# Gathering tokens for eight experts at a time in a two-layer mixture-of-experts trunk

## The chip, the cores and the metric

The kernel runs on one core of a Trainium2 chip. What is measured is the device time of one execution in microseconds (us): three runs of the kernel before took 750.36, 750.12 and 752.44 us, so the median is 750.36 us. One further execution was recorded by the hardware profiler; it took 750.05 us, of which 748.3 us lie between its first and its last instruction (the span). All times in the profile are counted from the start of that span.

A core has engines that run side by side, each with a queue of its own that it works through strictly in order: TensorE (PE in the profile: matmuls, into PSUM), VectorE (DVE) and ScalarE (ACT, both elementwise), GpSimd (POOL), and SyncE (SP), which here only issues transfers (DMA). Instructions of different engines wait for each other by semaphores.

## The reference

Two layers (l = 0, 1) act on 256 tokens of 1024 features in float32. With six modulation vectors made from a conditioning vector by a large product (`ada_w`), each layer does:

```
h = rmsnorm(x) * (1 + sc1) + sh1
x = x + g1 * (concat(three kinds of attention on h @ w_in) @ w_out)       # the mixer
h = rmsnorm(x) * (1 + sc2) + sh2
x = x + g2 * moe(h)                                                       # 16 experts
return rmsnorm(x)                                                         # after layer 1
```

The router picks one of four groups of experts for each token and the two best experts in it. The output of an expert is `(silu(h @ w_gate) * (h @ w_up) * gate) @ w_down`, with 512 inner features. All sixteen experts get tokens, so all their weights have to be read, some 200 MB of the 283.63 MB that the whole kernel moves.

## The kernel before

**Weights.** All large weights go by one SP queue, in an order fixed when the program is built (`Ring.fill`, L154), in units of 512 KB (a tile of 128x1024). Most units go into a ring of 29 tiles named `big`. A unit of the ring can be issued when the unit 29 places back in the ring has been released, that is, read for the last time by PE. Some units are put elsewhere: for units 21 to 26 of each layer's experts (`HALVES`) two tiles of the pool `w` are used, and for those in `LENT` a tile of the pool `k`. Units in other pools take no place in the ring. As SP issues in order, a unit that waits holds up all units behind it. At most eight transfers are under way at a time: a full queue makes SP wait for a transfer to end.

**The experts.** `moe` goes through the 16 experts as eight pairs (j = 0 to 7). A pair has eight units for its gate products, eight for up and eight for down. I count the units of one layer's experts r = 0, 1, 2, ...: gate of pair 0 is 0 to 7, up of pair 0 is 8 to 15, gate of pair 1 is 16 to 23, down of pair 0 is 24 to 31, up of pair 1 is 32 to 39 and so on. `first` (L1362) makes a quarter of a gate or up product and releases two units; `down` (L1408) does the same for the way back; `combine` (L1429) spreads the result to the tokens' rows. In a trace one float32 matmul is two records, so a `first` is eight records of L1362; the order lists count it as four.

**The gather.** Each expert has 64 places. `pos` says, for each token and expert, which place it has. `one_hot(b)` (L1304, DVE) makes a 0/1 matrix of 128 tokens x (4 experts x 64 places) for each half of the tokens. `gather(b, k2)` (L1328) multiplies the normed tokens, split into a rounded part `xhi` and a rest `xlo`, with it: the result for 2 of the 8 blocks k of 128 features fills one PSUM tile `t`. There are two such tiles. `modulate` then writes scale * t + shift into a `k` tile, for two blocks at a time alternately by ACT (L724) and DVE (L726). With four experts in a gather there are four gathers in a layer, at pairs 0, 2, 4 and 6. Two of their quarters stand ahead of the pair's first `first`, one between the first and the second and one between the second and the third.

**What sets the order.** Each engine works in the order in which the Python code emits its instructions, but for some pieces that are kept back on purpose (`issue_after`). Ahead of the experts the router's DVE instructions come in this order: `pos` (L1239), the one-hot matrix, the eight pieces of `xlo` (L1247), small ones for the gate weights, and the sum `g2rows` (L1297), from which `g2` (L562) makes the factor of the expert layer's output by two float32 matmuls. The mixer's steps follow a list (`MIX`, `TAIL`), where a letter d stands for a quarter of the product for one modulation vector (`one_unit`, L532, eight records), CF for a piece of attention kind C, AM for one of kind A, and W for a step of the output projection. The products of projections are three matmuls each (L718 to L720), on weights that ACT and DVE split first (L770, L775).

**The end.** The last pair's way back (`last`, L1443 and L1460) is cut into pieces. For the final norm, POOL multiplies x with the final gains (`weigh`, L1570), and after the norm's factor is known, DVE and ACT multiply by it (L1564, L1562); four transfers of 256 KB write the output.

Of the kernel before, what the change touches and what calls it, by code (L numbers as in the profile page):

```python
# [29 lines left out]
SCRATCH = 512  # L30
AHEAD = 2
HALVES = ((21, 27), (21, 27))
LENT = (((27, 32), (61, 62), (64, 65), (67, 68)),) * 2
NW = 17
A_START = 24

# [19 lines left out]

START = ["X c c R c c S00".split(), "S00 S01 X0 X1 a S02 X2 a X3 a a R a".split()]
TAIL = """
CT0 d CT1 d CF0 AM1 d d W0 CF1
BV0 BV1 W1 BV2 BV3 BO0 BV4 W2 BV5 CV0 W3 BO1 CV1 CV2 W4 CO0 W5 W6  # L60
"""
MIX = [("""
# [137 lines left out]
class Body:  # L200
# [20 lines left out]
    def setup(self):  # L221
        nc, a, const = self.nc, self.a, self.const
        cb = self.cb = const.tile([128, NCONST], F32, name="cb")
        nc.sync.dma_start(out=cb[:, 0:C_Z], in_=a["first"])
        self.load_x()
        self.ring.fill(2 * KT + 4)
        nc.sync.dma_start(out=cb[:, C_CAUSAL:C_CAUSAL2], in_=a["rest"])

        self.qb = const.tile([128, 512], F32, name="qb")
        nc.gpsimd.memset(self.qb, 0.0)  # L230
        for l in range(DEPTH):
            nc.gpsimd.dma_start(out=self.qb[l:128:32], in_=a["ada_b"][l])
# [12 lines left out]
        self.cact = cb[:, _AT["C"]]  # L245
        nc.scalar.activation(self.cact, self.cact, AF.Silu)
        cols = cb[:, _AT["COLS"]].rearrange("p (n k) -> p n k", k=KT)
        self.bcol = cols[:, 0:6 * DEPTH].rearrange("p (l v) k -> p l v k", l=DEPTH)
        self.gain = {nm: cols[:, 6 * DEPTH + DEPTH * i:6 * DEPTH + DEPTH * (i + 1)]
                     for i, nm in enumerate(("norm_mix_g", "norm_ffn_g"))}  # L250
        self.add = cb[:, _AT["ADD"]]
        self.pair = cb[:, _AT["PAIR"]]
        self.subg = cb[:, _AT["SUBG"]].rearrange("p (l d) -> p l d", l=DEPTH)
        self.sink = cb[:, _AT["SINK"]].rearrange("p (l d) -> p l d", l=DEPTH)
        self.wr = cb[:, _AT["WR"]].rearrange("p (l k g) -> p l k g", l=DEPTH, k=KT)
        self.rb = [cb[0:1, _AT["RB"]][:, 20 * l:20 * l + 20] for l in range(DEPTH)]
        self.tables(posi)
        self.later = True
# [58 lines left out]
    def lambdas(self):  # L317
# [8 lines left out]
        nc.vector.tensor_tensor(out=lam, in0=ls[:, 1], in1=ls[:, 0], op=OP.subtract)  # L326
        for l in range(DEPTH):
            nc.vector.tensor_scalar(lam[:, l:l + 1], lam[:, l:l + 1], -self.lambda_init(l), None, op0=OP.add)
        pl = self.pt.tile([128, 512], F32, name="t")
        nc.tensor.matmul(pl[:, 0:DEPTH], lhsT=self.ones[0:1], rhs=lam[0:1, :], start=True, stop=True)  # L330
# [119 lines left out]
    def ada_unit(self, l, q, i):  # L450
# [15 lines left out]
        else:  # L466
            nc.scalar.copy(rows[64:128], self.q[64:128])
            nc.vector.tensor_tensor(out=rows[0:64], in0=self.q[0:64], in1=self.qb[0:64], op=OP.add)
        self.pending.append(lambda: self.ada_columns(l, q, rows))

    def ada_columns(self, l, q, rows):
        nc = self.nc
# [83 lines left out]
    def g2(self, l):  # L556
# [338 lines left out]
    def mixer(self, l):  # L895
# [17 lines left out]

        if self.later:
            self.more_tables()


        def proj(u, g):
# [229 lines left out]
        for what in MIX[l]:  # L1148
# [11 lines left out]
                self.spread(l, int(n))  # L1160
            elif name == "L":
                if self.later:
                    self.lambdas()
                    self.later = False
            else:
                steps[name](int(n))
# [88 lines left out]
    def gates_of_tokens(self, l, dense, lg, l5, rank, og, tl):  # L1255
# [35 lines left out]
        if not dense:  # L1291
# [1 line left out]
            nc.gpsimd.tensor_copy(ghl[:, :, 0], gate)  # L1293
            nc.gpsimd.tensor_tensor(out=ghl[:, :, 1], in0=gate, in1=ghl[:, :, 0].bitcast(F32), op=OP.subtract)
            self.ghl = ghl
        self.g2rows = self.w()
        nc.vector.tensor_tensor(out=self.g2rows, in0=self.q, in1=self.qb, op=OP.add)  # L1297

    def one_hot(self, b):

        one = self.w(F32R).rearrange("p (t e s) -> p t e s", t=2, e=4)
        iota = self.cb[:, C_IOTA:C_IOTA + CAP].unsqueeze(1).to_broadcast([128, 4, CAP])
        for t in range(2):
            i = self.nc.vector.tensor_tensor(out=one[:, t], in0=iota, op=OP.is_equal,  # L1304
                                             in1=self.pos[:, t, 4 * b:4 * b + 4].unsqueeze(2).to_broadcast([128, 4, CAP]))
        self.hot[b] = one.rearrange("p t e s -> p t (e s)")
        return i


    def moe(self, l):  # L1310
        nc, ring = self.nc, self.ring
        hot = self.hot
        sh, sc, g = self.mod[l, 3], self.mod[l, 4], None
        xt, G, U, pts, gates, act = {}, {}, {}, {}, {}, {}

        def gather(b, k2):

            if k2 == 0:
                if b:
                    self.one_hot(b)  # L1320
                xt[b] = [self.wk.tile([128, 4, S], F32, name="k") for _ in range(2)]
            one = hot[b]
            p = self.pt.tile([128, 512], F32, name="t").rearrange("p (k s) -> p k s", k=2)
            for kk in range(2):
                n = 0
                for part in (self.xhi, self.xlo):
                    for t in range(2):
                        nc.tensor.matmul(p[:, kk], lhsT=part[t][:, 2 * k2 + kk], rhs=one[:, t],  # L1328
                                         start=(n == 0), stop=(n == 3))
                        n += 1  # L1330
            for kk in range(2):
                self.modulate(xt[b][k2 // 2][:, 2 * (k2 % 2) + kk], p[:, kk], sc, sh, 2 * k2 + kk, 1 - k2 % 2)

        def places(j):

            p = self.pt.tile([128, 512], F32, name="t")
            hf = hot[j // 2][:, :, 128 * (j % 2):128 * (j % 2) + 128]
# [14 lines left out]
        def first(kind, store, j, hh):  # L1352

            if hh == 0:
                store[j] = self.ps.tile([128, 512], F32, name="s")
            x = xt[j // 2]
            w = [ring.take2((kind, l, 2 * j + u, hh)) for u in range(2)]
            for kk in range(2):
                k = 2 * hh + kk
                for u in range(2):  # L1360
                    c = (j % 2) * 128 + 64 * u
                    nc.tensor.matmul(store[j][64 * u:64 * u + 64, :], lhsT=x[k // 4][:, k % 4, c:c + 64],  # L1362
                                     rhs=w[u][kk], start=(k == 0), stop=(k == KT - 1))
            ring.done(2)

        def gates_of(j, between=None):

            if j % 2:
                first("gate", G, j, 0)
                first("gate", G, j, 1)  # L1370
                if between:
                    between()
            else:
                gather(j // 2, 0)
                gather(j // 2, 1)
                first("gate", G, j, 0)
                gather(j // 2, 2)
                if between:
                    between()
                first("gate", G, j, 1)  # L1380
                gather(j // 2, 3)
            first("gate", G, j, 2)
            first("gate", G, j, 3)
            silu(j)
# [48 lines left out]
        def last(j):  # L1433
# [18 lines left out]
            def combined(d, c0, n):  # L1452
# [12 lines left out]
                        nc.vector.tensor_tensor(out=self.x[t][:, c], in0=self.x[t][:, c], in1=o[t], op=OP.add)  # L1465
                else:
                    self.key = nc.vector.tensor_tensor(out=self.xt[:, :, c], in0=self.xt[:, :, c], in1=o3, op=OP.add)
                if l + 1 == DEPTH:
                    self.weigh(c)
                i = {0: 0, 512: 2, 768: 1}[c0]  # L1470
                for t in range(2):
# [22 lines left out]
                    next(self.starting)  # L1494

        for j in range(8):
            gates_of(j, (lambda: down_in(j - 1)) if j else None)
            if j == 0:
                self.g2(l)
                g = self.mod[l, 5]  # L1500
            if j:
                parts = down(j - 1)
            places(j)
            for hh in range(4):
                first("up", U, j, hh)
            product(j)
# [47 lines left out]
    def final(self, out):  # L1554
        nc = self.nc
        r = self.rstds(self.squares(), False)
        for t in range(2):
            for hf in range(2):
                c = slice(512 * hf, 512 * hf + 512)
                y = self.y[t][:, c]  # L1560
                if t and hf:
                    nc.scalar.activation(y, y, AF.Copy, scale=r[t])  # L1562
                else:
                    nc.vector.tensor_scalar(y, y, r[t], None, op0=OP.mult)  # L1564
                (nc.scalar if hf else nc.sync).dma_start(out=out[0, 128 * t:128 * t + 128, c], in_=y)

    def weigh(self, c):

# [12 lines left out]
    def forward(self, out, dense):  # L1581
# [14 lines left out]
                self.moe(l)  # L1596
        if dense:
            self.load_fng()
            self.weigh(slice(0, D))
        self.final(out)  # L1600


# [49 lines left out]
```

## Time and profile before

| | |
|---|---|
| median of three runs | 750.36 us |
| profiled execution | 750.05 us |
| its span | 748.3 us |
| mean granted clock of TensorE | 0.986 of full speed |
| PE busy | 711.3 us (95%) |
| DVE, ACT, POOL busy | 342.1, 211.5, 65.3 us |
| moved | 283.63 MB, mean 379 GB/s |
| transfers of 512 KB, issue to landing | 10.2 us median |

The table is an account over the whole span. Layer 0's mixer fills it up to about 166 us, its experts up to about 381 us; layer 1's mixer follows up to about 523 us and its experts up to about 737 us. The rate at which data moves, in 40 slices of the span, tells the stages apart better than any sum: it is near 409 GB/s in most slices and well below it in a few.

### The profile page before, as it was taken

What the parts mean: (1) busy time and instruction counts of PE and PEld (TensorE: products, weight loads), DVE (VectorE), ACT (ScalarE), POOL (GpSimd) and SP (SyncE); (2) the same over time, 40 slices, a digit from 0 to 9 for tenths busy, and PEclk for the clock granted to TensorE, in tenths of its full rate; (3) what the DMA queues carried; (4) which work ended last, traced back from release to release, by engine and by line L of the source; (5) the groups of instructions that cost most, each with busy time, mean ns of one, the idle gap of its engine ahead of it and who ended that gap; (6) DMA issues with size and microseconds to landing.
All of it is one profiled execution on the core that took longest, in us unless ns stands there. A gap on an engine that the chain in (4) does not pass through costs nothing. (4 is left out here: it accounts for less than half of the span.)

```text
span 748.3 us, 10676 instructions
## 1 busy us (share of the span) xinstructions
PE 711.3 (95%) x3790; PEld 368.8 (49%) x3790; DVE 342.1 (46%) x940; ACT 211.5 (28%) x482; POOL 65.3 (9%) x89
## 2 busy tenths in 40 slices
PE   6899899989999999999999999898999999999993
PEld 2565675754353353343337677575435335344341
DVE  4587697373133133223358879538213312332234
ACT  2345345532111111111134645544211011112011
POOL 1010224101000000000001122400100000000002
PEclk9999999999999999999999999999999999999997
DMA  9999999999999999999999996869989999999991
GB/s 352 409 410 406 406 410 408 408 386 409 391 357 409 409 410 409 408 409 410 397 408 409 406 406 210 335 209 401 327 339 396 409 409 409 409 409 409 409 379 63
DMA packets 82745, 283.63 MB, mean 379 GB/s; under 512 B 9198, under 2 KB 9327, under 8 KB 82684
## 3 DMA queue, kind: packets, MB, share of 16 engines
q1 hardware_dynamic: 82186, 282.33, 96.1%
q8 instruction: 32, 0.52, 0.3%
q10 hardware_dynamic: 434, 0.53, 0.2%
q14 instruction: 29, 0.24, 0.1%
q0 software_dynamic: 64, 0.02, 0.0%
HBM read 281.78 MB, written 1.06 MB: 378 GB/s over the span
## 5 line engine op out<-in xcount | busy, mean ns | idle before, releaser
L1362 PE MATMUL s<-big,k 128*64 128x512 f32 x976 | 228.2, 598 | 0.0
L1362 PEld LDWEIGHTS s<-big,k 128*64 128x64 f32 x976 | 67.4, 136 | 118.5 <-issue 103.2
L1414 DVE SCALAR_TENSOR_TENSOR w<-acc,gs,g 128x512 f32<-128x512 f32 x28 | 21.0, 751 | 155.3 <-PE acc L1408 153.8
L1408 PE MATMUL acc<-big,w 128*64 128x512 f32 x384 | 84.4, 592 | 0.0
L775 DVE TENSOR_TENSOR k<-big,k 128x1024 fp32r<-128x1024 f32 (+1 forms) x56 | 66.4, 1192 | 14.5 <-ACT k L770 10.2
L718 PE MATMUL acc<-k 128*128 128x512 f32 (+1 forms) x176 | 70.0, 397 | 3.0 <-ACT k L707 2.0
L720 PE MATMUL acc<-k 128*128 128x512 f32 (+1 forms) x176 | 66.6, 379 | 0.0
L719 PE MATMUL acc<-k 128*128 128x512 f32 (+1 forms) x176 | 66.3, 377 | 0.0
L770 ACT CAST k<-big 128x1024 fp32r<-128x1024 f32 (+1 forms) x56 | 54.2, 985 | 37.3 <-PE acc L719 27.5
L1408 PEld LDWEIGHTS acc<-big,w 128*64 128x64 f32 x384 | 27.6, 137 | 54.8 <-issue 52.2
L1393 DVE TENSOR_TENSOR w<-w,s 128x512 f32<-128x512 f32 x16 | 11.0, 688 | 84.3 <-PE s L1362 84.3
L718 PEld LDWEIGHTS acc<-k 128*128 128x128 f32 x176 | 33.9, 193 | 18.2 <-issue 6.1
L1418 ACT CAST w<-w 128x512 fp32r<-128x512 f32 x28 | 17.3, 618 | 89.8 <-DVE w L1414 89.8
L1328 PEld LDWEIGHTS t<-w,k 128*128 128x128 f32 x256 | 32.8, 190 | 16.3 <-issue 9.9
L835 ACT ACTIVATE w<-w,nm 128x128 f32<-128x128 f32 (+1 forms) x80 | 35.4, 444 | 15.9 <-DVE nm L833 15.8
L1399 ACT COPY w<-t 128x512 f32<-128x512 f32 x16 | 9.4, 585 | 107.9 <-PE t L803 107.9
L1328 PE MATMUL t<-w,k 128*128 128x256 f32 x256 | 37.6, 291 | 1.7 <-DVE w L1304 1.7
L724 ACT ACTIVATE k<-t,mod,mod 128x256 f32<-128x256 f32 x32 | 16.3, 561 | 79.1 <-PE t L1328 79.1
L720 PEld LDWEIGHTS acc<-k 128*128 128x128 f32 x176 | 33.7, 191 | 7.7 <-DVE k L891 1.6
L719 PEld LDWEIGHTS acc<-k 128*128 128x128 f32 x176 | 33.9, 193 | 5.0
L803 PE MATMUL t<-cb,w 128*128 128x128 f32 x224 | 34.1, 281 | 1.4 <-ACT w L860 1.4
L1431 DVE TENSOR_TENSOR x<-x,acc 128x512 f32<-128x512 f32 x56 | 34.9, 681 | 0.2
(269 smaller groups left out, 852.6 us busy)
## 6 DMA issues: line engine op xcount, KB each, us to landing
big<-in_expert_w_up_dram SPq DMA_DIRECT2D x126, 512.0 KB, 10.2
big<-in_expert_w_gate_dram SPq DMA_DIRECT2D x118, 512.0 KB, 10.2
big<-in_expert_w_down_dram SPq DMA_DIRECT2D x108, 512.0 KB, 10.1
big<-in_ada_w_dram SPq DMA_DIRECT2D x80, 512.0 KB, 10.2
big<-in_w_in_dram SPq DMA_DIRECT2D x32, 512.0 KB, 10.2
big<-in_ada_w_first_dram SPq DMA_DIRECT2D x16, 512.0 KB, 10.2
big<-in_w_out_dram SPq DMA_DIRECT2D x16, 512.0 KB, 9.7
w<-in_expert_w_down_dram SPq DMA_DIRECT2D x20, 256.0 KB, 6.8
```

The lines of the kernel that those rows point to most:

```text
L718: self.nc.tensor.matmul(p, lhsT=xh, rhs=wh, start=start, stop=False)
L719: self.nc.tensor.matmul(p, lhsT=xh, rhs=wl, start=False, stop=False)
L720: self.nc.tensor.matmul(p, lhsT=xl, rhs=wh, start=False, stop=stop)
L770: nc.scalar.copy(hi, w)
L775: nc.vector.tensor_tensor(out=lo, in0=w, in1=hi.bitcast(F32), op=OP.subtract)
L803: self.nc.tensor.transpose(p[:, i], b, self.ident)
L835: nc.scalar.activation(e[:, h], e[:, h], AF.Exp, bias=nm[:, g:g + 1], scale=scale, accum_out=sm[:, g:g + 1])
L1328: nc.tensor.matmul(p[:, kk], lhsT=part[t][:, 2 * k2 + kk], rhs=one[:, t], start=(n == 0), stop=(n == 3))
L1362: nc.tensor.matmul(store[j][64 * u:64 * u + 64, :], lhsT=x[k // 4][:, k % 4, c:c + 64], rhs=w[u][kk], start=(k == 0), stop=(k == KT - 1))
L1408: nc.tensor.matmul(ps[hf][64 * u:64 * u + 64, :], lhsT=act[j][:, f, 64 * u:64 * u + 64], rhs=w[u][hf], start=(f == 0), stop=(f == 3))
L1414: nc.vector.scalar_tensor_tensor(out=ds[-1], in0=p, scalar=gates[j], in1=g[:, 512 * hf:512 * hf + 512], op0=OP.mult, op1=OP.mult)
L1431: nc.vector.tensor_tensor(out=self.x[t][:, c], in0=self.x[t][:, c], in1=p, op=OP.add)
```

## The change

`one_hot(b)` now makes the matrix for eight experts (two instructions of 128x512), and `gather(b, k)` fills a PSUM tile with one block k of features for all eight. There are two gathers in a layer, at pairs 0 and 4, of eight blocks each: four blocks stand ahead of the pair's first `first`, two between the first and the second, two between the second and the third. `modulate` now takes one block of 128x512, even blocks by ACT and odd blocks by DVE. The gathered tokens take four `k` tiles where they took two, and `LENT` gives units 30 and 31 back to the ring. The 0/1 rows that `places` needs are made for each pair by `rows_of`. `g2` works with two rounded parts (four matmuls in place of two float32 ones). In the mixer, the columns of a modulation vector (`ada_columns`) come one stage later, the lambdas of attention kind A are computed earlier, and in `TAIL` one d moves ahead of CF0. At the end, POOL weighs only the first 512 columns, DVE does the rest in one instruction per half of the tokens, and two transfers of 512 KB write the output.

```
-LENT = (((27, 32), (61, 62), (64, 65), (67, 68)),) * 2
+LENT = (((27, 30), (61, 62), (64, 65), (67, 68)),) * 2
-CT0 d CT1 d CF0 AM1 d d W0 CF1
+CT0 d CT1 d d CF0 AM1 d W0 CF1
...
-        self.add = cb[:, _AT["ADD"]]
+        self.add = const.tile([128, 2 * DEPTH], F32R, name="add")
+        nc.gpsimd.tensor_copy(self.add, cb[:, _AT["ADD"]])
...
-        self.pending.append(lambda: self.ada_columns(l, q, rows))
+        self.pending.append(lambda: self.pending.append(lambda: self.ada_columns(l, q, rows)))
...
         if self.later:
             self.more_tables()
+            self.lambdas()
...
-            nc.tensor.matmul(p, lhsT=self.add[:, 2 * l + h:2 * l + h + 1].to_broadcast([128, 128]), rhs=self.g2rows,
-                             start=True, stop=True)
+            for n, part in enumerate(self.g2rows):
+                nc.tensor.matmul(p, lhsT=self.add[:, 2 * l + h:2 * l + h + 1].to_broadcast([128, 128]), rhs=part,
+                                 start=(n == 0), stop=(n == 1))
...
-        self.g2rows = self.w()
-        nc.vector.tensor_tensor(out=self.g2rows, in0=self.q, in1=self.qb, op=OP.add)
+        rows = self.w()
+        nc.vector.tensor_tensor(out=rows, in0=self.q, in1=self.qb, op=OP.add)
+        self.g2rows = [self.w(F32R) for _ in range(2)]
+        nc.scalar.copy(self.g2rows[0], rows)
+        nc.vector.tensor_tensor(out=self.g2rows[1], in0=rows, in1=self.g2rows[0].bitcast(F32), op=OP.subtract)
...
+        def gather(b, k):
+            if k == 0:
+                xt[b] = []
+            if k % 2 == 0:
+                xt[b].append(self.wk.tile([128, 2, 512], F32, name="k"))
+            p = self.pt.tile([128, 512], F32, name="t")
+            n = 0
+            for part in (self.xhi, self.xlo):
+                for t in range(2):
+                    nc.tensor.matmul(p, lhsT=part[t][:, k], rhs=hot[b][t], start=(n == 0), stop=(n == 3))
+                    n += 1
+            self.modulate(xt[b][k // 2][:, k % 2], p, sc, sh, k, 1 - k % 2)
...
+            ks = range(KT) if j % 4 == 0 else ()
+            for k in ks[0:4]:
+                gather(j // 4, k)
+            first("gate", G, j, 0)
+            for k in ks[4:6]:
+                gather(j // 4, k)
+            if between and ks:
+                between()
+            first("gate", G, j, 1)
+            if between and not ks:
+                between()
+            for k in ks[6:8]:
+                gather(j // 4, k)
             first("gate", G, j, 2)
             first("gate", G, j, 3)
...
-                if l + 1 == DEPTH:
+                if l + 1 == DEPTH and c0 == 0:
                     self.weigh(c)
...
+            y = self.y[t]
+            nc.scalar.activation(y[:, c0], y[:, c0], AF.Copy, scale=r[t])
+            nc.vector.scalar_tensor_tensor(out=y[:, c1], in0=self.x[t][:, c1], scalar=r[t], in1=self.fng[:, c1],
+                                           op0=OP.mult, op1=OP.mult)
+            nc.sync.dma_start(out=out[0, 128 * t:128 * t + 128, :], in_=y)
```

The first place is DVE at the start of layer 0's experts in the kernel before. The names `k<-t` are modulations of gathered tokens, `w<-cb,pos` is the one-hot matrix and `w<-s,qb` the sum for g2.

```order
314 L1304 TENSOR_TENSOR w<-cb,pos 128x256 x2
315 L1247 SCALAR_TENSOR_TENSOR k<-x,newton,k 128x256 x8
316 L1260 TENSOR_REDUCE mp<-pos 128x1
319 L1267 TENSOR_SCALAR o_1883<-rank 128x32
320 L1297 TENSOR_TENSOR w<-s,qb 128x512
321 L726 TENSOR_SCALAR k<-t,mod_4_1429,mod_3_891 128x256 x2
325 L1270 TENSOR_REDUCE m_1882<-g_1888 128x8
326 L1282 RECIPROCAL w_1899<-w_1899 128x8
327 L726 TENSOR_SCALAR k<-t,mod_4_1429,mod_3_891 128x256 x2
```

DVE's first modulation stands behind the sum for g2; it is that of blocks 2 and 3. The same place of DVE after the change:

```order
316 L1318 TENSOR_TENSOR w<-cb,pos 128x512 x2
317 L1254 SCALAR_TENSOR_TENSOR k<-x,newton,k 128x256 x8
318 L1267 TENSOR_REDUCE mp<-pos 128x1
321 L1274 TENSOR_SCALAR o_1882<-rank 128x32
322 L1304 TENSOR_TENSOR w<-s,qb 128x512
323 L1268 TENSOR_SCALAR ovf<-mp 128x1
324 L732 TENSOR_SCALAR k<-t,mod_4_1421,mod_3_918 128x512
327 L1307 TENSOR_TENSOR w<-w 128x512
329 L732 TENSOR_SCALAR k<-t,mod_4_1421,mod_3_918 128x512
330 L1289 RECIPROCAL w_1898<-w_1898 128x8
331 L732 TENSOR_SCALAR k<-t,mod_4_1421,mod_3_918 128x512 x2
```

The first modulation still stands behind the sum for g2, and it is now that of block 1. On PE the same place reads, before:

```order
416 L1328 MATMUL t<-w,k 128x256 x16
417 L1362 MATMUL s<-big,k 64x512 x4
418 L1328 MATMUL t<-w,k 128x256 x8
419 L1362 MATMUL s<-big,k 64x512 x4
422 L562 MATMUL acc<-w,cb 128x512 x2
```

After, PE has as many matmuls, of twice the width:

```order
416 L1338 MATMUL t<-w,k 128x512 x16
417 L1376 MATMUL s<-big,k 64x512 x4
418 L1338 MATMUL t<-w,k 128x512 x8
419 L1376 MATMUL s<-big,k 64x512 x4
422 L568 MATMUL acc<-w,add 128x512 x4
```

The last row of each is g2: two float32 matmuls before, four of rounded parts now. The third place is SP in layer 1, from unit 24 on, where units go to the pools `w`, `k` and the ring `big`. Before:

```order
90 L154 DMA w<-in_expert_w_gate_dram 128x512 x6
91 L154 DMA w<-in_expert_w_down_dram 128x512 x6
92 L154 DMA k<-in_expert_w_down_dram 128x1024 x5
93 L154 DMA big<-in_expert_w_up_dram 128x1024 x8
94 L154 DMA big<-in_expert_w_gate_dram 128x1024 x8
```

After:

```order
91 L154 DMA w<-in_expert_w_gate_dram 128x512 x6
92 L154 DMA w<-in_expert_w_down_dram 128x512 x6
93 L154 DMA k<-in_expert_w_down_dram 128x1024 x3
94 L154 DMA big<-in_expert_w_down_dram 128x1024 x2
95 L154 DMA big<-in_expert_w_up_dram 128x1024 x8
```

Units 30 and 31 have moved into the ring, so each ring unit from 32 up to 60 waits for a unit two places later in the ring than before.

## Rows read from the trace of the kernel before

**Rows 1.** The page: rate of the transfers in 40 slices of the span.

```profile
GB/s 352 409 410 406 406 410 408 408 386 409 391 357 409 409 410 409 408 409 410 397 408 409 406 406 210 335 209 401 327 339 396 409 409 409 409 409 409 409 379 63
```

**Rows 2.** Busy time by stretch, layer 1: PE, PEld, DVE, ACT, POOL, clock, DMA, GB/s.

```profile
440.00:500.00 60.00, 56.92 (x377) 41.59 (x376) 38.51 (x140) 31.75 (x85) 15.51 (x16) 0.97 0.74 269
500.00:565.00 65.00, 62.44 (x353) 29.73 (x352) 24.62 (x71) 15.16 (x32) 2.37 (x11) 1.00 0.93 352
565.00:728.00 163.00, 163.00 (x797) 68.19 (x796) 47.54 (x91) 22.54 (x43) 1.48 (x2) 1.00 1.03 407
```

**Rows 3.** SP's waits from 570 to 722 us: total, times, longest.

```profile
SPq L154 <- DMA big<-in_expert_w_up_dram: 34.4, 39, 1.5
...
SPq L154 <- PE s L1362: 14.7, 15, 3.8
```

**Rows 4.** Timeline of SP near the end: start, us, what.

```profile
700.99 9.26 SPq L154 DMA_DIRECT2D big<-in_expert_w_up_dram  x8
```

**Rows 5.** Transfers from 600 to 712 us: size, median us to landing.

```profile
big<-in_expert_w_up_dram SPq DMA_DIRECT2D x32, 512.0 KB, 10.2
```

**Rows 6.** Timeline of PE: pair 7's up in layer 1.

```profile
715.07 7.09 PE L1362 MATMUL s<-big,k 128*64 128x512 f32 x32
```

**Rows 7.** Timeline of PE: where layer 1 starts.

```profile
381.79 2.14 PE L457 MATMUL acc<-big,cb 128*32 128x512 f32 x8
```

**Rows 8.** Timeline of PE: first and third `first` of layer 0's experts.

```profile
170.59 1.94 PE L1362 MATMUL s<-big,k 128*64 128x512 f32 x8
...
176.62 1.94 PE L1362 MATMUL s<-big,k 128*64 128x512 f32 x8
```

**Rows 9.** Timeline of DVE at the same place.

```profile
167.24 0.76 DVE L1304 TENSOR_TENSOR w<-cb,pos 128x256 fp32r<-128x256 f32 x2
167.92 3.25 DVE L1247 SCALAR_TENSOR_TENSOR k<-x,newton,k 128x256 fp32r<-128x256 f32 x8
...
171.45 0.68 DVE L1297 TENSOR_TENSOR w<-s,qb 128x512 f32<-128x512 f32 x1
172.05 0.98 DVE L726 TENSOR_SCALAR k<-t,mod,mod 128x256 f32<-128x256 f32 x2
```

**Rows 10.** Timeline of PE, layer 0: a later gather, and a `combine`.

```profile
213.43 2.07 PE L1328 MATMUL t<-w,k 128*128 128x256 f32 x16
...
217.29 1.22 PE L1328 MATMUL t<-w,k 128*128 128x256 f32 x8
...
239.86 2.11 PE L1429 MATMUL acc<-w 128*128 128x512 f32 x8
```

**Rows 11.** Groups of PE's instructions from 178 to 183 us: busy, mean ns.

```profile
L562 PE MATMUL acc<-w,cb 128*128 128x512 f32 x4 | 2.0, 618 | 0.0
```

**Rows 12.** Timeline of SP: units 60, 61, 62 of layer 0; 62 of layer 1.

```profile
195.72 0.33 SPq L154 DMA_DIRECT2D big<-in_expert_w_up_dram  x1
200.63 0.33 SPq L154 DMA_DIRECT2D k<-in_expert_w_up_dram  x1
206.41 0.80 SPq L154 DMA_DIRECT2D big<-in_expert_w_up_dram  x2
...
559.33 0.80 SPq L154 DMA_DIRECT2D big<-in_expert_w_up_dram  x2
```

**Rows 13.** Timeline of PE: the end of pair 0's down in layer 0.

```profile
200.00 4.03 PE L1408 MATMUL acc<-k,w 128*64 128x512 f32 x17
```

**Rows 14.** PE's waits in layer 0's mixer, 47 to 167 us.

```profile
PE t L330 <- DVE lam L328: 0.7, 1, 0.7
```

**Rows 15.** Timeline of PE in layer 1's mixer, at the step CF0.

```profile
467.76 1.06 PE L532 MATMUL acc<-big,cb 128*32 128x512 f32 x8
470.62 0.72 PE L1074 MATMUL s<-w 64*128 64x128 f32 x8 [1.80 <-DVE w L1068]
...
471.64 3.31 PE L532 MATMUL acc<-big,cb 128*32 128x512 f32 x16
```

**Rows 16.** The end: transfers of the output, median us to landing.

```profile
out_dram<-k SPq DMA_DIRECT2D x2, 256.0 KB, 3.3
```

More of the change, by code (lines that the diff above doesn't have):

```diff
@@ L328, in lambdas, with spread_lambdas @@
             nc.vector.tensor_scalar(lam[:, l:l + 1], lam[:, l:l + 1], -self.lambda_init(l), None, op0=OP.add)
+        self.lam = lam
+    def spread_lambdas(self):
+        nc, const = self.nc, self.const
         pl = self.pt.tile([128, 512], F32, name="t")
-        nc.tensor.matmul(pl[:, 0:DEPTH], lhsT=self.ones[0:1], rhs=lam[0:1, :], start=True, stop=True)
+        nc.tensor.matmul(pl[:, 0:DEPTH], lhsT=self.ones[0:1], rhs=self.lam[0:1, :], start=True, stop=True)
         self.nlam = const.tile([128, DEPTH], F32, name="nlam")
@@ L1162, in mixer @@
                 if self.later:
-                    self.lambdas()
+                    self.spread_lambdas()
                     self.later = False
@@ L1295, in gates_of_tokens, with hot_of @@
             self.ghl = ghl
-        self.g2rows = self.w()
-        nc.vector.tensor_tensor(out=self.g2rows, in0=self.q, in1=self.qb, op=OP.add)
+        rows = self.w()
[3 more added lines that the diff above has]
+        nc.vector.tensor_tensor(out=self.g2rows[1], in0=rows, in1=self.g2rows[0].bitcast(F32), op=OP.subtract)
     def one_hot(self, b):
-        one = self.w(F32R).rearrange("p (t e s) -> p t e s", t=2, e=4)
-        iota = self.cb[:, C_IOTA:C_IOTA + CAP].unsqueeze(1).to_broadcast([128, 4, CAP])
+        self.hot[b] = [self.w(F32R) for t in range(2)]
         for t in range(2):
-            i = self.nc.vector.tensor_tensor(out=one[:, t], in0=iota, op=OP.is_equal,
-                                             in1=self.pos[:, t, 4 * b:4 * b + 4].unsqueeze(2).to_broadcast([128, 4, CAP]))
-        self.hot[b] = one.rearrange("p t e s -> p t (e s)")
-        return i
+            i = self.hot_of(self.hot[b][t], t, 8 * b, 8)
+        return i
+    def hot_of(self, out, t, e0, n):
+        iota = self.cb[:, C_IOTA:C_IOTA + CAP].unsqueeze(1).to_broadcast([128, n, CAP])
+        return self.nc.vector.tensor_tensor(out=out.rearrange("p (e s) -> p e s", e=n), in0=iota, op=OP.is_equal,
+                                            in1=self.pos[:, t, e0:e0 + n].unsqueeze(2).to_broadcast([128, n, CAP]))
     def moe(self, l):
@@ L1313, in moe, with rows_of @@
         sh, sc, g = self.mod[l, 3], self.mod[l, 4], None
[L1314 to L1332, printed above, removed]
+        xt, G, U, pts, gates, act, pair = {}, {}, {}, {}, {}, {}, {}
+        def gather(b, k):
[10 more added lines that the diff above has]
+            self.modulate(xt[b][k // 2][:, k % 2], p, sc, sh, k, 1 - k % 2)
+        def rows_of(j):
+            hf = self.w(F32R)[:, 0:S].rearrange("p (t c) -> p t c", t=2)
+            for t in range(2):
+                self.hot_of(hf[:, t], t, 2 * j, 2)
+            pair[j] = hf
         def places(j):
             p = self.pt.tile([128, 512], F32, name="t")
-            hf = hot[j // 2][:, :, 128 * (j % 2):128 * (j % 2) + 128]
+            hf = pair.pop(j)
             for t in range(2):
@@ L1355, in first @@
                 store[j] = self.ps.tile([128, 512], F32, name="s")
-            x = xt[j // 2]
+            x = xt[j // 4]
             w = [ring.take2((kind, l, 2 * j + u, hh)) for u in range(2)]
@@ L1360, in first @@
                 for u in range(2):
-                    c = (j % 2) * 128 + 64 * u
-                    nc.tensor.matmul(store[j][64 * u:64 * u + 64, :], lhsT=x[k // 4][:, k % 4, c:c + 64],
+                    c = (j % 4) * 128 + 64 * u
+                    nc.tensor.matmul(store[j][64 * u:64 * u + 64, :], lhsT=x[k // 2][:, k % 2, c:c + 64],
                                      rhs=w[u][kk], start=(k == 0), stop=(k == KT - 1))
@@ L1366, in gates_of @@
         def gates_of(j, between=None):
[L1368 to L1381, printed above, removed]
+            ks = range(KT) if j % 4 == 0 else ()
[11 more added lines that the diff above has]
+                gather(j // 4, k)
             first("gate", G, j, 2)
@@ L1496, in moe @@
         for j in range(8):
+            if j:
+                rows_of(j)
             gates_of(j, (lambda: down_in(j - 1)) if j else None)
@@ L1502, in moe @@
                 parts = down(j - 1)
+            else:
+                rows_of(j)
             places(j)
+            if j == 3:
+                self.one_hot(1)
             for hh in range(4):
@@ L1556, in final @@
         r = self.rstds(self.squares(), False)
+        c0, c1 = slice(0, 512), slice(512, 1024)
         for t in range(2):
[L1558 to L1565, printed above, removed]
+            y = self.y[t]
[3 more added lines that the diff above has]
+            nc.sync.dma_start(out=out[0, 128 * t:128 * t + 128, :], in_=y)
     def weigh(self, c):
@@ L1598, in forward @@
             self.load_fng()
-            self.weigh(slice(0, D))
+            self.weigh(slice(0, 512))
         self.final(out)
```

## The prediction

> **What bounds the kernel now.** I first read the rate of the transfers by slice. It is at about 409 GB/s nearly throughout and falls below 350 at one place alone, slices 24 to 26, 28 and 29 counted from 0 [rows 1], which is layer 1's mixer and the start of its experts. There the ring is full and SP waits for releases; the stretches by engine say the same: 269 GB/s from 440 to 500 us, 352 up to 565, and 407 from 565 to 728, where PE is busy 163 of 163 us [rows 2]. So in the experts both PE and the transfers look like the bound. What tells them apart is who waits for whom. SP's waits from 570 to 722 us are mostly for its own queue of eight to get a place, 34.4 us for up's units alone, and 14.7 for releases by L1362 [rows 3]: the queue is full. And the units arrive ever closer to their use. The eight units of pair 7's up in layer 1 are issued from 700.99 to about 710.2 us [rows 4]; the last pair of them starts at 709.9, lands 10.2 us later [rows 5], at 720.1, and its `first` begins after three quarters of the 7.09 us from 715.07 [rows 6], at 720.4. The lead that the ring gave has been eaten up just where the kernel ends. In layer 0 the lead ends at layer 1's start: L457 needs 2.14 us for eight matmuls at 381.79 [rows 7], where the like eight of L532 need 1.06 [rows 15], since it waits within them for its second unit. So in each layer there is a line of transfers that runs full from about unit 62 of the experts to the layer's end. When unit 62 is issued, 206.41 us and 559.33 us [rows 12], decides when that line ends, and what PE saves behind that point waits at its end. The time before unit 62 is set by releases, thus by how early the experts start and by what stands between them.
>
> **The opening of the experts.** Before, the first `first` starts at 170.59 us [rows 8]; its tokens were modulated by ACT. Now blocks 0 to 3 of all eight experts come first, and with two PSUM tiles the gather of block 3 must wait until block 1 has been modulated, by DVE. On DVE that stands behind the whole router tail. Step by step from 167.24 [rows 9]: two one-hot instructions of 128x256 took 0.76, so of 128x512 I count 1.25 (to 168.5); the eight xlo pieces 3.25 (171.7); the small ones from 171.17 to 171.45, 0.28 (172.0); the sum for g2 0.6 to 0.68 (172.7); one more small one 0.1; the modulation of 128x512, from 0.49 to 0.54 for half of it, about 0.8 (173.6). Then four matmuls of 512 columns: eight of L1429 took 2.11 [rows 10], some 0.21 each with 0.3 of filling, so with the handover 1.0. The first `first` starts at 174.6, 4.0 later. Between it and the third stand two blocks twice, eight matmuls of 512 columns in place of 256: 2.0 against some 1.2 [rows 10], so 0.85 more each time: the third starts 5.7 later than 176.62 [rows 8]. Then g2: four float32 records of two matmuls took 2.0 [rows 11], four rounded ones of 512 columns take 1.15, which gives back 0.85. From pair 0's up on, releases come 4.8 later. The bounds: 2.5, if DVE did not hold up block 3 (one-hot, 16 matmuls of 3.4 and 0.2 of handover give 172.3, so +1.7, +1.7 for the next two gathers, -0.85 for g2), and 5.5 if all of DVE's rows stretch a little.
>
> A row of the trace shows what held before: DVE's first modulation ran at 172.05, after PE had begun the first `first` [rows 8, 9], because it was not needed for it. The Trainium skill, page Perfetto Trace Analysis, section Optimizing Scalar/DVE Operations, says that where these engines are not saturated but cause bubbles on others, breaking up their instructions may let work be done sooner. The change goes the other way. By that rule the opening gets later; a sum without it would be that with 2.5.
>
> **LENT.** Units 30 and 31 return to the ring, so units 32 to 60 wait for a unit two places later; for 62 on the releaser is the same as before. Unit 60 was issued at 195.72, 61 at 200.63, 62 at 206.41 [rows 12]. Now 59 and 60 wait for the end of pair 0's down (204.0 before, [rows 13]) and stand directly ahead of 62. Three units in front of it, at 1.28 us each (512 KB at 409 GB/s), in the 2.4 us between the two releases put its landing back by 1.4 at most. But before, the line after unit 62 had small holes where it waited for releases behind pair 2's gather, which now goes away (slice 11 stands at 357, [rows 1]). I let the two cancel: bounds 0 and +1.4. So each layer's line is 4.8 later, plus or minus what the mixer ahead of it gives.
>
> **What PE saves later.** Four gathers cost 32 matmuls of 256 columns each, 2.07 + 2 x 1.2 with overlap some 4.3 [rows 10], 17.2 in all; two of 32 x 512 cost 7.7 each, 15.4. This saving of 1.8 lies behind unit 62 and ends in the wait for the last units. I count it at nothing; if the transfers were no cover, it would count fully.
>
> **Layer 0's mixer.** Lambda's wait on PE was 0.7 [rows 14] and goes, as its DVE work is done earlier; the columns a stage later change little, for the projection's next weights are split by DVE at the same time. I take -0.6 on the start of layer 0's experts, bounds -2.0 and +0.6.
>
> **Layer 1's mixer.** PE stood 1.80 before L1074 at 470.62, and afterwards 16 records of L532 took 3.31 where eight had taken 1.06 [rows 15]; the stretch's mean granted clock is 0.97 [rows 2], and the slow part is here. One d moved ahead of it fills 1.0 of the hole, and 8 of the 16 remain behind: at the normal clock the next step starts 3.31 - 1.06 = 2.2 earlier, though the hole itself only becomes shorter. From there PE leads on. I take -2.1, bounds -2.5 and 0.
>
> **The end.** The last transfers have 512 KB where 256 KB landed after 3.3 [rows 16]; 256 KB more at 409 GB/s are 0.64. Against that stands one issue less per half of the tokens, and for it DVE's fused instruction, which has one input more. I take +0.6, bounds -0.5 and +1.5. The rest (`rows_of`, one more cast and difference for g2) runs beside L1362 on engines that are idle half of the time: nothing; if it delayed a modulation of pair 4, it would be about 0.4.
>
> **The sum.** On the profiled execution's 750.05 (span 748.3 and 1.75 around it): layer 0's line +4.8, its mixer -0.6, layer 1's mixer -2.1, layer 1's line +4.8, the end +0.6, together +7.5: 757.5. The median of the runs is 0.3 above the profiled execution, which is within what I can work out; I leave it at 757.5.
>
> **The rivals.**
> 1. PE sets the end. Then only PE's own account counts. Per layer that is the hold-up by DVE, 4.8 - 2.5 = 2.3, less the gathers' 1.8 (which hold the broader blocks of the opening) and less g2's 0.85: -0.35. With two layers, both mixers and the end: 750.05 - 0.7 - 0.6 - 2.1 + 0.6 = 747.2. For it: PE is busy 163 of 163 us in [rows 2]. Against it: the slack of 0.3 us at 720 us. It decides if units 176 to 183 of layer 1 still land before PE wants them. The Trainium skill, page Perfetto Trace Analysis, section Matmuls, says that larger matmuls are more efficient than smaller ones when possible; that rule alone would lead to this rival. Chance 0.16.
> 2. DVE does not hold up the gather: the opening costs 2.5 in place of 4.8, and the sum is 750.05 + 2.5 - 0.6 - 2.1 + 2.5 + 0.6 = 752.9. For it: nothing but that the times on DVE are estimates. Against: the order on DVE is fixed. Chance 0.16.
> 3. The later opening is absorbed, as the holes before unit 62 (slices 10, 11, 28 and 29, [rows 1]) take it up; what remains is the mixers and the end, less a little: 749 to 751. Chance 0.10.
>
> **How the numbers follow.** The forecast has 0.58. A difference of 0.3%, 2.25 us, is about what a measurement of this kernel can tell from none. Faster by more than that is rival 1 and a little of rival 3: 0.17. Within it is most of rival 3 and somewhat under half of rival 2: 0.16. Slower is the forecast and the rest of rival 2: 0.67. The forecast's own range is 754 to 761.5 (both layers' 1.4 for LENT and no gain in layer 1's mixer above; half of the hold-up below). The range for 8 in 10 goes down to 750, which leaves out rival 1, and up to 761.5.
>
> **What will show it.** In the changed profile the first `first` of each layer should start about 7.4 us after the one-hot matrix does (3.4 before), after a wait of PE for DVE's modulation; unit 62 should be issued about 4.8 us later against it; L457 at layer 1's start and the last `first`s should wait for transfers; in layer 1 the 16 records at 471.64 should fall apart, with no slow clock. If PE never waits for a transfer in pairs 6 and 7, the forecast fails by rival 1; if the first `first` starts under 6 us after the one-hot matrix, by rival 2.

## The result, and the profile after

The changed kernel takes 759.63 us in the median (758.24 to 761.31), the kernel before 750.24 us in the same rounds. The ratio is 1.0125, with a 95% interval of 1.0104 to 1.0146: 1.25% slower. The profiled execution took 759.21 us, its span is 757.4 us; against the profiled execution of before that is +9.16 us.

First the rate of the transfers, on the page of the kernel after, in 40 slices of its span.

```profile
GB/s 349 409 409 407 407 409 409 408 395 250 392 369 408 410 410 408 409 410 410 400 405 408 407 408 223 334 258 324 218 376 405 408 409 409 410 408 410 408 396 76
```

Slice 9 has fallen to 250, where it was 409 [rows 1]: that is 170 to 189 us, the start of layer 0's experts, where SP now waits for the first releases (from 165 to 190 us up to 9.5 us for one by L1376; before, 3.2 by L1362). In layer 1 slice 28, 530 to 549 us, shows the same: 218, where it was 327. The busy time by stretch in layer 1 (PE, PEld, DVE, ACT, POOL, clock, share of DMA, GB/s):

```profile
440.00:500.00 60.00, 56.28 (x376) 42.22 (x376) 43.87 (x153) 33.19 (x88) 18.17 (x18) 1.00 0.79 291
500.00:565.00 65.00, 61.91 (x339) 32.36 (x337) 25.47 (x71) 17.11 (x33) 2.36 (x11) 0.97 0.87 317
565.00:575.00 10.00, 10.00 (x48) 3.90 (x45) 4.17 (x10) 1.51 (x3) 0.00 (x0) 1.00 0.90 337
575.00:738.00 163.00, 162.35 (x733) 62.98 (x733) 45.96 (x89) 19.84 (x35) 2.36 (x2) 1.00 1.03 408
```

From 575 us on the transfers run as full as before from 565 [rows 2], so they reach that point some 10 us later. SP's waits from 580 to 732 us (total, times, longest):

```profile
SPq L154 <- DMA big<-in_expert_w_up_dram: 35.3, 40, 1.6
...
SPq L154 <- PE s L1376: 2.5, 9, 0.4
```

Releases by `first` (L1376 now) have almost ceased to hold up SP: 2.5 us, where L1362 had 14.7 [rows 3]; all releases by PE together fell from 20.4 to 7.3. So PE frees the tiles before the queue wants them, and near the end it is PE that waits for transfers. SP's timeline, and then PE's, near pair 7's up:

```profile
710.60 9.29 SPq L154 DMA_DIRECT2D big<-in_expert_w_up_dram  x8
```

```profile
721.90 5.11 PE L1376 MATMUL s<-big,k 128*64 128x512 f32 x18
727.22 2.35 PE L1376 MATMUL s<-big,k 128*64 128x512 f32 x8 [0.21 <-DMA big<-in_expert_w_up_dram]
729.79 1.93 PE L1376 MATMUL s<-big,k 128*64 128x512 f32 x6 [0.22 <-DMA big<-in_expert_w_up_dram]
```

What was one row of 32 without a gap [rows 6] falls apart into pieces with a transfer as the releaser, at the rhythm of the line (two units, 2.56 us). The same eight units of up are issued at 710.60, 9.6 us later than before [rows 4].

The opening of layer 0's experts on PE:

```profile
168.42 3.86 PE L1338 MATMUL t<-w,k 128*128 128x512 f32 x12 [1.10 <-DVE w L1318]
173.84 1.19 PE L1338 MATMUL t<-w,k 128*128 128x512 f32 x4 [1.57 <-DVE k L732]
174.97 1.94 PE L1376 MATMUL s<-big,k 128*64 128x512 f32 x8
...
182.81 3.65 PE L1376 MATMUL s<-big,k 128*64 128x512 f32 x16
```

And on DVE:

```profile
167.58 1.29 DVE L1318 TENSOR_TENSOR w<-cb,pos 128x512 fp32r<-128x512 f32 x2
168.79 3.25 DVE L1254 SCALAR_TENSOR_TENSOR k<-x,newton,k 128x256 fp32r<-128x256 f32 x8
...
172.32 0.69 DVE L1304 TENSOR_TENSOR w<-s,qb 128x512 f32<-128x512 f32 x1
172.93 0.15 DVE L1268 TENSOR_SCALAR ovf<-mp 128x1 f32<-128x1 f32 x1
172.99 0.81 DVE L732 TENSOR_SCALAR k<-t,mod,mod 128x512 f32<-128x512 f32 x1
```

The gather of block 3 stands still for 1.57 us until DVE has modulated block 1, which on DVE stands behind the pieces of xlo, the small ones and the sum for g2. The first `first` starts 7.39 us after the one-hot matrix, against 3.35 [rows 8, 9]. The opening of layer 1's experts on PE, and its stretch (columns as above):

```profile
525.32 5.21 PE L1338 MATMUL t<-w,k 128*128 128x512 f32 x12 [1.10 <-DVE w L1318]
530.68 1.20 PE L1338 MATMUL t<-w,k 128*128 128x512 f32 x4 [0.15 <-DVE ovf L1268]
531.81 1.94 PE L1376 MATMUL s<-big,k 128*64 128x512 f32 x8
```

```profile
525.00:530.00 5.00, 4.55 (x11) 3.26 (x12) 5.00 (x16) 0.99 (x3) 0.20 (x1) 0.67 0.87 347
```

Here the same 12 matmuls took 5.21 us in place of 3.86: the mean granted clock was 0.67, and most of them start 0.43 us apart, where 0.23 is usual at full clock (the levels are 1.2 and 2.4 GHz). So PE was ready for block 3 only 0.15 us before DVE, which modulated block 1 from 529.83 to 530.63 us, let it go on. The first `first` comes 7.33 us after the one-hot matrix (524.48, shown below), as in layer 0: the low clock ran beside DVE's hold-up and cost nothing more.

SP's timeline at units 56 to 62 of layer 0, and at unit 62 of layer 1:

```profile
198.41 11.84 SPq L154 DMA_DIRECT2D big<-in_expert_w_up_dram  x5
210.30 0.42 SPq L154 DMA_DIRECT2D k<-in_expert_w_up_dram  x1
211.81 0.80 SPq L154 DMA_DIRECT2D big<-in_expert_w_up_dram  x2
...
568.65 0.80 SPq L154 DMA_DIRECT2D big<-in_expert_w_up_dram  x2
```

The five of the first row now end just behind the end of pair 0's down (209.4 us on PE), and unit 62 is issued 5.40 us later in layer 0 and 9.32 later in layer 1 [rows 12]. Layer 1 starts 6.22 us later [rows 7], and it again waits for its units:

```profile
388.01 2.16 PE L462 MATMUL acc<-big,cb 128*32 128x512 f32 x8
```

The mixer of layer 1 at CF0:

```profile
474.39 1.92 PE L537 MATMUL acc<-big,cb 128*32 128x512 f32 x16
477.65 0.71 PE L1081 MATMUL s<-w 64*128 64x128 f32 x8 [1.33 <-DVE w L1075]
...
478.66 1.06 PE L537 MATMUL acc<-big,cb 128*32 128x512 f32 x8
```

The 16 slow records [rows 15] are gone. DVE's one-hot matrix of layer 1 stands, in the kernel before and after, at

```profile
520.16 0.76 DVE L1304 TENSOR_TENSOR w<-cb,pos 128x256 fp32r<-128x256 f32 x2
```

```profile
524.48 1.29 DVE L1318 TENSOR_TENSOR w<-cb,pos 128x512 fp32r<-128x512 f32 x2
```

that is 4.32 later, after a layer that started 6.22 later.

### The profile page after: what moved, and what is told of

Same layout as the page of the kernel before. It is cut to its first block, busy times and chain, and to the rows that moved or that the text cites. A ratio compares the mean times of both kernels' runs of the same rounds, so it can differ in the third digit from the quotient of the medians.

```text
span 757.4 us, 10392 instructions
## 1 busy us (share of the span) xinstructions
PE 717.3 (95%) x3662; PEld 362.9 (48%) x3662; DVE 346.4 (46%) x949; ACT 210.5 (28%) x469; POOL 62.9 (8%) x86
## 5 line engine op out<-in xcount | busy, mean ns | idle before, releaser
L1376 PE MATMUL s<-big,k 128*64 128x512 f32 x976 | 231.9, 598 | 0.9 <-DMA big<-in_expert_w_up_dram 0.9
L1376 PEld LDWEIGHTS s<-big,k 128*64 128x64 f32 x976 | 69.3, 136 | 127.4 <-issue 115.1
L1421 PE MATMUL acc<-big,w 128*64 128x512 f32 x400 | 91.7, 594 | 0.6 <-DMA big<-in_expert_w_down_dram 0.6
L1421 PEld LDWEIGHTS acc<-big,w 128*64 128x64 f32 x400 | 29.8, 137 | 60.1 <-issue 53.7
L1338 PE MATMUL t<-w,k 128*128 128x512 f32 x128 | 36.3, 424 | 4.2 <-DVE w L1318 2.2
L809 PEld LDWEIGHTS t<-cb,w 128*128 128x128 f32 x224 | 25.3, 143 | 20.4 <-issue 16.0
L1338 PEld LDWEIGHTS t<-w,k 128*128 128x128 f32 x128 | 23.9, 197 | 18.7 <-issue 9.7
```

What stands on the lines that cost most here:

```text
L809: self.nc.tensor.transpose(p[:, i], b, self.ident)
L1338: nc.tensor.matmul(p, lhsT=part[t][:, k], rhs=hot[b][t], start=(n == 0), stop=(n == 3))
L1421: nc.tensor.matmul(ps[hf][64 * u:64 * u + 64, :], lhsT=act[j][:, f, 64 * u:64 * u + 64], rhs=w[u][hf], start=(f == 0), stop=(f == 3))
```

## The experiments

The theory was that of the prediction: each layer ends with a line of transfers that starts when unit 62 is issued. What PE does ahead of that counts fully, what it does behind it counts nothing. The rivals were PE's own account (all of PE's work counts alike), and other parts of the change as the cause.

**Fewer gathers behind unit 62.** From the kernel before, the gathers of pairs 4 and 6 left out:

```
-            if j % 2:
+            if j % 2 or j >= 4:
+                if j % 2 == 0:
+                    self.one_hot(j // 2)
+                    xt[j // 2] = xt[1]
```

> The kernel before without the gathers of pairs 4 and 6 in both layers; the experts of these pairs read the tokens gathered for pair 2 (this part of the computation is left out). PE has 4.3 us less to do twice in each layer, all behind unit 62. If the line of transfers sets each layer's end (my theory), the time stays at 750 within 1 us, and PE waits for transfers in the last pairs. If PE sets the end, it falls by 17 us, to 733.

Measured: ratio to before 0.9989 (0.9969 to 1.0010). Some 17 us less of PE's work change nothing. PE's waits from 640 to 735 us in this kernel:

```profile
PE s L1362 <- DMA big<-in_expert_w_up_dram: 0.8, 4, 0.2
PE acc L1411 <- DMA big<-in_expert_w_down_dram: 0.6, 3, 0.2
```

```profile
720.85 2.35 PE L1362 MATMUL s<-big,k 128*64 128x512 f32 x8 [0.22 <-DMA big<-in_expert_w_up_dram]
```

The waits named are short, but around them eight records of L1362 take 2.35 us in place of 1.94, so most of the waiting is inside the busy time. PE's busy time as a whole says the same:

```profile
PE 710.5 (95%) x3662; PEld 357.3 (48%) x3662; DVE 334.6 (45%) x924; ACT 203.9 (27%) x466; POOL 65.4 (9%) x89
```

It was 711.3 us before: 128 matmul records are gone, and the time shows as busy all the same. PE's account is refuted.

**More gathering ahead of it.** From the kernel before, pair 0's gather done twice:

```
+                for again in range(1 if b else 2):
...
+                            nc.tensor.matmul(p[:, kk], lhsT=part[t][:, 2 * k2 + kk], rhs=one[:, t],
```

> The kernel before with the 32 matmuls of pair 0's gather done twice in each layer (the second time overwrites the first), nothing else changed: 3.4 us more for PE ahead of unit 62, where the kernel with fewer gathers had 8.6 us less behind it. My theory: each microsecond ahead of unit 62 counts once in each layer, as the line of transfers starts that much later: the first `first` 1.7 us later, the third 3.4, unit 62 as much, the time 6 to 7 us up, 757. Rival: the transfers have room, and PE's lead in the later pairs makes up for it: under 2 us.

Measured: 1.0085 (1.0056 to 1.0114), that is some +6.4 us, or 3.2 per layer, where 3.4 had been expected. In its profile, PE's third `first` and SP's unit 62 of layer 0:

```profile
180.46 3.65 PE L1363 MATMUL s<-big,k 128*64 128x512 f32 x16
```

```profile
210.25 0.80 SPq L154 DMA_DIRECT2D big<-in_expert_w_up_dram  x2
```

Against the one-hot matrix (165.89) both come 5.2 us later than before; some of this is a lower clock in the one execution that was profiled (0.72 from 165 to 170 us, before 1.00). The delay then passes through: counted from the start of the span, unit 62 of layer 0 is issued 3.84 us later than before and layer 1 starts 3.84 later; with layer 1's own delay its unit 62 comes 9.23 later, and the span is 9.0 longer. PE's account would also give some 6 us for added work; it is the run with fewer gathers that excludes it. Together they show that the same kind of work that could be dropped for nothing behind unit 62 costs its time ahead of it. Work added behind unit 62 was not tried; the slack of 0.3 us at the end of layer 1's up speaks against its being free.

**The two halves of the change.** The gather of eight with its rows and LENT put into the kernel before (e6), and the changed kernel with these taken back (e5):

> The kernel before with the gather of eight, its rows for places and LENT alone. My theory: all of the loss is here, and the rest of the change hid a part of it: each layer's line 6 to 7 us later (g2's 0.85 is not there), 762 to 764. Rival: the loss needs the other parts as well, above all the second sum for g2 in DVE's queue: 757 or less.

> The changed kernel with the gather of four experts, its one-hot matrices and LENT as before; the other parts of the change stay (g2 in rounded parts, one d ahead of CF0, columns and lambda moved, the final weighing). My theory: g2 gives 0.85 us per layer ahead of unit 62, so 1.7 in all, the d 1.9, the rest nothing: 746.5, with the first `first` 3.4 us after the one-hot matrix as before. Rival: the other parts carry a share of the loss (columns a stage later, fused final weighing), and the time is 750 or more.

Measured: 1.0172 (1.0149 to 1.0196) and 0.9947 (0.9927 to 0.9968). Together they make 1.0118, the changed kernel's 1.0125 within its interval. All of the loss is in the gather and LENT; the rest gains.

**LENT alone.**

```
-LENT = (((27, 32), (61, 62), (64, 65), (67, 68)),) * 2
+LENT = (((27, 30), (61, 62), (64, 65), (67, 68)),) * 2
```

> The kernel before with LENT of the changed one alone: units 30 and 31 go through the ring. My theory: units 59 and 60 are issued at the end of pair 0's down, about 204.1 us in layer 0 where 60 was issued at 195.7; unit 62 is still issued at 206.4 but lands 1.5 us later, and part of that is given back by holes further on: 0 to +1.5 us per layer, 750 to 753 in all. Rival: the two units cost a full starvation of some 3 us per layer, 756.

Measured: 1.0011 (0.9994 to 1.0027), +0.8 us, not told from no change. SP's timeline of layer 0 shows the wait that was expected, five units of up that end at 206.9 us:

```profile
194.74 12.19 SPq L154 DMA_DIRECT2D big<-in_expert_w_up_dram  x5
206.97 0.42 SPq L154 DMA_DIRECT2D k<-in_expert_w_up_dram  x1
207.85 0.80 SPq L154 DMA_DIRECT2D big<-in_expert_w_up_dram  x2
```

Unit 62 (207.85) comes 1.44 us later than before, but so does the third `first` (178.05 against 176.62), after a gather that ran at a low clock in this execution; LENT did not move it. LENT is the smaller part of the 12.9 us that gather and LENT cost together.

**DVE's hold-up.** In the changed kernel, block 1 of each layer's first gather modulated by ACT:

```
-            self.modulate(xt[b][k // 2][:, k % 2], p, sc, sh, k, 1 - k % 2)
+            self.modulate(xt[b][k // 2][:, k % 2], p, sc, sh, k, int(k % 2 == 0 or (b, k) == (0, 1)))
```

> The changed kernel, with one modulation moved: block 1 of the first gather of each layer is modulated by ScalarE (ACT) and not by VectorE (DVE). If the hold-up by DVE is what makes the opening late (my theory), PE's wait of 1.57 us before the gather of block 3 goes, and the rest of its late start too: the first `first` comes about 5 us after the one-hot matrix in place of 7.4, unit 62 is issued 2.4 us earlier in each layer, and the time falls by 4 to 5 us, to about 755. If only the width of the gathers counts and DVE's queue does not, the first `first` and the time stay within 1 us. If the later units wait for LENT alone, the first `first` moves but the time does not.

Measured: 1.0086 (1.0057 to 1.0114) to before, against 1.0125 for the changed kernel: some 2.9 us better, less than expected, and the two intervals just overlap, so the 2.9 is rough. PE at the opening of layer 0 and of layer 1 in this kernel:

```profile
168.69 5.96 PE L1338 MATMUL t<-w,k 128*128 128x512 f32 x16 [1.10 <-DVE w L1318]
174.58 1.94 PE L1376 MATMUL s<-big,k 128*64 128x512 f32 x8
...
525.61 4.80 PE L1338 MATMUL t<-w,k 128*128 128x512 f32 x16 [1.10 <-DVE w L1318]
530.34 1.94 PE L1376 MATMUL s<-big,k 128*64 128x512 f32 x8
```

The wait for DVE's modulation is gone, and in layer 1 the first `first` comes 5.57 us after the one-hot matrix (524.77), 1.8 sooner than with the hold-up. In layer 0 it comes only 0.7 sooner, as the same 16 matmuls took 1.2 us longer than in layer 1. The stretch's clock goes with it (columns as above):

```profile
170.00:175.00 5.00, 5.00 (x16) 3.60 (x17) 4.67 (x17) 2.98 (x6) 0.55 (x3) 0.70 0.83 329
```

At 0.23 us from start to start and full clock, 16 matmuls would take some 3.9 us, by estimate. Layer 1's 4.80 is more, as they also wait for the pieces of xlo, which come from DVE at 0.4 us each: the third and the fourth matmul start 0.06 and 0.05 us after the first two pieces are done. So taking away one wait shows the next. And the hold-up is worth 1.8 us only where the clock is full: at the clock of the changed kernel's layer 1 its removal would have given, by estimate, little more than the 0.15 us that PE waited there.

This kernel also shows what the width costs without the hold-up. Against the changed kernel with the gather and LENT of before (0.9947) it is some 10.4 us longer, of which LENT alone accounts for about 0.8.

**The gains alone.** The d ahead of CF0 in the kernel before, and then the d with g2 in rounded parts:

```
-CT0 d CT1 d CF0 AM1 d d W0 CF1
+CT0 d CT1 d d CF0 AM1 d W0 CF1
```

> The kernel before with the changed TAIL alone (one d ahead of CF0). My theory: layer 1's mixer ends 1.9 to 2.2 us earlier, since the hole of 1.80 us before L1074 is partly filled and the 16 records of L532 that took 3.31 us fall apart; it carries to the end, since the experts' line of transfers is set by when the experts start: 748.0. Rival: the mixer's later steps wait for DVE anyway and the time stays at 750.

> The kernel before with two parts of the change, g2 in rounded parts and the d ahead of CF0. My theory: these two are all that gains, 746.5, the same as with the columns, lambda and the final weighing on top. Rival: the columns and lambda give 0.7 to 2 us more, and this one is that much slower than the kernel with all but the gather.

Measured: 0.9976 (0.9960 to 0.9993) and 0.9931 (0.9909 to 0.9953), the latter 746.36 us in the median. PE in the first of the two:

```profile
468.23 1.92 PE L532 MATMUL acc<-big,cb 128*32 128x512 f32 x16
471.10 0.71 PE L1074 MATMUL s<-w 64*128 64x128 f32 x8 [0.94 <-DVE w L1068]
...
472.11 1.06 PE L532 MATMUL acc<-big,cb 128*32 128x512 f32 x8
```

The hole is down from 1.80 to 0.94 us and the clock holds (1.00 from 470 to 475 us, 0.70 before). The first kernel's gain of some 1.8 us is the 2 expected; in its profiled execution layer 1's mixer is 2.84 us shorter, but the clock then falls at the opening of layer 1's experts (0.66 from 520 to 525 us), and the third `first` comes 1.5 us later against the one-hot matrix. g2 takes 1.2 us in place of 2.0 in the second kernel:

```profile
L564 PE MATMUL acc<-w,add 128*128 128x512 f32 x4 | 1.2, 418 | 0.0
```

This kernel beats the one before (by 0.7%) and the changed one (by 1.9%). Columns, lambda and the final weighing on top of it (0.9947) give nothing that can be told.

## Why the prediction was right

The time, 759.6 us, lies in the range and 2.1 us above the forecast. By its own steps, from the profiled executions:

| step | forecast | measured |
|---|---|---|
| layer 0's mixer | -0.6 | +0.34 (one-hot at 167.58) |
| opening to unit 62, layer 0 | +4.8 | +5.06 (5.40 - 0.34) |
| unit 62 to layer 1's start | 0, at most +1.4 | +0.82 (6.22 - 5.40) |
| layer 1's mixer | -2.1 | -1.90 (4.32 - 6.22) |
| opening to unit 62, layer 1 | +4.8 | +5.00 (9.32 - 4.32) |
| unit 62 to the end of up, layer 1 | 0, at most +1.4 | +0.29 (9.61 - 9.32) |
| the end | +0.6 | -0.45 (9.16 - 9.61) |
| sum | +7.5 | +9.16 |

The mechanism held. The line of transfers as the bound of both layers was shown by taking PE's work away behind unit 62 (0.9989) and adding it ahead (1.0085). The DVE hold-up was there where it was forecast, and the first `first` came 7.39 and 7.33 us after the one-hot matrix where 7.4 had been worked out; but as a wait of PE it shows in layer 0 alone (1.57 us, and 0.15 in layer 1, where a low clock hid the rest).

Some sizes were off. The gain in layer 0's mixer did not come: the one-hot matrix stood between 165.4 and 168.0 us in the profiles of all these kernels, and the 0.34 is within that. LENT and the holes behind it did not cancel; together they cost 1.1. And the end gained a little: the larger transfers landed after 3.7 us in place of 3.3, so 0.4 later and not 0.64, and other steps there became shorter. These misses are not all of one sign (+0.94, +1.11 and -1.05, with +0.46 for the two openings and +0.20 for layer 1's mixer); that the sum is off by no more than 1.66 us is in part luck. The bounds of the range, too, are not the sums that the prediction gives for them: both of LENT's 1.4 and no gain in layer 1's mixer make 762.4 and not 761.5, half of the hold-up off makes 755.2 and not 754. The measured time lies inside either way.

The hold-up itself was put too high at 2.3 per layer: with it gone the first `first` came 1.8 earlier in layer 1, 5.57 us after the one-hot matrix, a bound that I had put at 5.1. In it the 16 matmuls were put at 3.4 us, while they need some 3.9 at full clock, and the waits for xlo were left out. The Trainium skill, page Perfetto Trace Analysis, section Optimizing Scalar/DVE Operations, says that breaking up instructions of Scalar or Vector may allow work to be completed sooner where these engines are not saturated but cause bubbles on others. The wait of 1.57 us on PE agrees that DVE caused a bubble; breaking up an instruction was not tried. Moving the one instruction to ACT was worth about 2.9 of the 9.4 us, though (1.25%); most of the rest is width: twice the gather ahead of the first releases.

The larger matmuls were no gain here. The Trainium skill, page Perfetto Trace Analysis, section Matmuls, says that larger matmuls are more efficient than smaller ones, when possible. On PE the traces agree: the gathers' records fall in number from 256 to 128 and in busy time from 37.6 to 36.3 us. But that is a net figure, as is the 1.8 us per layer that the prediction counted as lying behind unit 62. By the prediction's own times, 5.2 us per layer are saved behind unit 62 (one gather of 7.7 in place of three of 4.3), where they are worth nothing, and 3.4 are added ahead of it, where they count.

What stays open is how the loss of 12.9 us for gather and LENT divides further: the interval of the run with LENT alone allows it anything from 0 to 2 us, the hold-up's 2.9 is rough, and no run widened the gather with nothing else.

## What to carry to other kernels

Where a ring of weights runs ahead of the work, ask of each saved or added microsecond on which side of the first starved transfer it lies: two kernels with work added and removed on the two sides (here +6.4 us and nothing) settle it in one go. Batching more work into one step ahead of the first release cost its full width here, although the total shrank. And small gains in the same change (here 0.7%) can hide behind a loss; taking the change apart finds them.

## What I had not expected

The granted clock of TensorE falls at the opening of the experts in some executions and not in others. The same 16 gather matmuls of the same shape took 5.96 us in layer 0 and 4.80 in layer 1 of one run, with a mean clock of 0.70 from 170 to 175 us in the former and of 1.00 from 525 to 530 in the latter; in the kernel with LENT alone the 16 of 256 columns took 4.11 us where they had 2.85 before, and its clock stood at

```profile
167.00:171.00 4.00, 3.23 (x13) 2.77 (x14) 3.97 (x11) 0.81 (x2) 0.00 (x0) 0.74 1.03 410
171.00:175.00 4.00, 4.00 (x21) 2.15 (x19) 2.36 (x12) 0.42 (x2) 0.41 (x2) 0.84 0.73 292
```

Such a stretch stands ahead of unit 62, so by the theory it counts fully, unless another wait covers it as in layer 1 of the changed kernel. It is a likely part of the spread of 5 us between executions of the kernel before: 747.21 us at a mean clock of 0.987, 752.88 at 0.983. From 165 to 170 us PE is busy 3.1 of the 5 us both in the changed kernel, where the clock held (1.00), and in the one with block 1 on ACT, where it fell (0.96, and then 0.70): what decides was not found.

At the end, DVE's two sums of one element (L1475) took 0.79 us in the kernel before, while POOL weighed 256-column pieces, and 0.35 in the one after, where POOL had nothing to do:

```profile
736.83 0.79 DVE L1475 TENSOR_TENSOR ss<-ss 128x1 f32<-128x1 f32 x2
```

```profile
746.47 0.35 DVE L1488 TENSOR_TENSOR ss<-ss 128x1 f32<-128x1 f32 x2
```

That is as much as the 0.45 that the end gained, but it is not the only step that moved: from DVE's last pass to the first output transfer it is 0.81 us in place of 0.51, and from there to the end of the span 7.13 in place of 7.59. That POOL is the reason for the 0.79 was not tried.
